# RWKV recurrence: scan states and values in two four-chunk tiles, bonus values in another pool, value stores issued by ScalarE

## The chip, the cores and the metric

The kernel runs on one core of a Trainium2 chip. The metric is device time of one launch in microseconds (us); lower is better. The core has a matrix engine (TensorE, called PE below), three engines for elementwise work (VectorE = DVE, ScalarE = ACT, GpSimd = POOL) and SyncE (SP), which here does nothing but issue DMAs. ACT can issue DMAs too. Each engine works through its own list of instructions in order and waits where a semaphore says so. A time comes with the granted TensorE clock, in parts of full speed.

## The reference

Two layers, 512 tokens, model width 1024, float32. Layer 0 has an RWKV-7 mixer, layer 1 a gated spatial unit (SGU); each is followed by a SwiGLU FFN. The change lies in the recurrence of the RWKV mixer, which runs over 16 heads of width 64:

```python
    def step(S, inp):                       # S: value x key, per head
        r_t, w_t, k_t, v_t, a_t, b_t = inp
        sa = jnp.einsum('bhij,bhj->bhi', S, a_t)
        S = (S * w_t[:, :, None, :]
             + sa[..., None] * b_t[:, :, None, :]
             + v_t[..., None] * k_t[:, :, None, :])
        y = jnp.einsum('bhij,bhj->bhi', S, r_t)
        return S, y
...
    mu = jnp.mean(y, axis=-1, keepdims=True)
    var = jnp.mean(jnp.square(y - mu), axis=-1, keepdims=True)
    y = (y - mu) * lax.rsqrt(var + GN_EPS)
    y = y * gn_w.reshape(H, N).astype(f32) + gn_b.reshape(H, N).astype(f32)
    y = y + jnp.sum(r_h * k_h * r_k.astype(f32), axis=-1, keepdims=True) * v_h
    y = y.reshape(B, T, D).astype(x.dtype)
    return (y * g) @ w_o
```

The last term before the gate, the sum over a head of r, k and r_k times the value, is called the bonus.

## The kernel before

Sixteen heads are four blocks of four heads; the 512 tokens are eight chunks of 64. For a block b the steps are: P and E (projections to r, k and the decay), F (the "front": products inside a chunk, PE lines 861 and 875, masked), B (the "back": the inverse of a 64 x 64 triangle per chunk and head; its forward substitution is a long chain of small DVE operations, lines 906 and 908, between two block transposes, LX at line 892 and Dn/Dt at lines 911 and 912), S (the scan over the eight chunks, lines 981 to 1025) and N (the "finish": group norm, bonus, output gate). V is the value projection in four column groups, lines 704 to 726. The list PLAN gives the order in which the steps are written, "P0 E0 P1 E1 P2 E2 P3 E3 X0 F0 B0 F1 V0 V1 V2 V3 B1 S0 F2 S1 F3 N0 B2 N1 B3 S2 N2 S3 N3"; a scheduler then lays the instructions of neighbouring steps into one another on every engine, by its own estimate of times and by what memory is free. So a change of a tile's place, or of the engine that issues a DMA, can move instructions that it does not name.

The value projection copies each PSUM result to a tile vev on ACT (line 724) and stores it to the array Vd in DRAM (line 725, 8 stores of 256 KB). Vd is read in two layouts. The scan reads it per chunk: a tile su holds, in its two halves of 64 partitions, the state of a head and the values of the chunk under it, so that one product applies both; its state half is written from PSUM us by DVE for one head of a pair (line 1007) and by ACT for the other (line 1010), its value half is loaded by two DMAs (line 990). The tiles su rotate through 4 buffers. The bonus reads Vd by tokens (line 1048) into a tile that shares two buffers (tag hn) with the Dn of the back and the squares of the group norm; DVE multiplies it by the bonus factor (line 1052), PE transposes it (vt, line 1055), ACT adds a bias and makes ob (line 1057). ob then takes the normalised Y (yt, line 1080) and the gate (lines 204 and 1084) and goes to DRAM as od (line 1094), from where the output projection loads it as oraw (line 1138), splits it to oT and multiplies (acc, line 204).

Weights are multiplied as a pair of roundings, whi (ACT cast, line 179) and wlo (DVE, line 180). The gate's weights g2h and g2l are made the same way from a load g (line 744); g2x (line 1069) comes from three small loads g2r (line 1066). The pool xp has four buffers of one size, given out by xslot; Y, the split input of the projections and the residual x share it. e2 gives out another pool of seven.

Of the kernel before, what the change touches and what calls it, by code (L numbers as in the profile page):

```python
# [7 lines left out]
F32 = mybir.dt.float32  # L8
# [5 lines left out]
P = 128  # L14
# [3 lines left out]
TT = T // P  # L18
H2 = 8
C = 64  # L20
# [110 lines left out]
class Trunk:  # L131
# [394 lines left out]
    def rwkv(self, x0):  # L526
        nc, i, tc = self.nc, self.i, self.tc
        v, a, g = nc.vector, nc.scalar, nc.gpsimd
        mm = nc.tensor.matmul
        with ExitStack() as ctx:  # L530
            ep = ctx.enter_context
            rp = ep(tc.tile_pool(name="rp", bufs=1))
            dp = ep(tc.tile_pool(name="dp", bufs=1, space=bass.MemoryType.DRAM))
            Vd = dp.tile([T, D], F32, name="Vd")
# [4 lines left out]
            def e(name, shape=(P, T), dt=F32):  # L539
                return rp.tile(list(shape), dt, name=name, tag="e", bufs=2)  # L540
# [4 lines left out]
            def e2(name, shape=(P, 2, T), dt=F32):  # L545
                return rp.tile(list(shape), dt, name=name, tag="e2", bufs=E2)

            def s4(name, shape, dt=F32):
                return self.slot(shape, dt, name)

            def xslot(name, shape, dt=F32):
                return self.xp.tile(shape, dt, name=name, tag="x", bufs=TT)
# [31 lines left out]
            h = [s4("h", [P, 2, 513]) for _ in range(4)]  # L584
# [3 lines left out]
            for tt in range(TT):  # L588
                hn = e2("hn", (P, D))
# [47 lines left out]
            q2 = range(2)  # L637
# [70 lines left out]
            def v_proj(xs, qts):  # L708

                for qt in qts:  # L710
                    cols = slice(qt * 256, qt * 256 + 256)
                    acc = [self.pb("v") for _ in range(2)]
                    for u in range(2):
                        hi, lo = self.weight(wrkv[2].rearrange("(u j p) n -> u p j n", p=P, j=4)[u][:, :, cols])
                        for j in range(4):
                            kt = 4 * u + j
                            for tt in range(TT):
                                tok = slice(tt * P, (tt + 1) * P)
                                self.mm3(acc[tt // 2][:, (tt % 2) * 256:(tt % 2) * 256 + 256],
                                         (xs[kt][:, 0, tok], xs[kt][:, 1, tok]), (hi[:, j, :], lo[:, j, :]),  # L720
                                         kt == 0 and tt % 2 == 0, kt == KT - 1 and tt % 2 == 1)
                    for n in range(2):
                        t = e("vev")
                        a.copy(t, acc[n])
                        nc.sync.dma_start(out=Vd.rearrange("(n j p) f -> n p j f", p=P, j=2)[n][:, :, cols],
                                          in_=t.rearrange("p (j f) -> p j f", j=2))

            fv = lambda n, p: self.vec[n][:, p:p + 1]
# [252 lines left out]
            def scan(b, o, then=None):  # L981

                MV, pc = o["MV"], o["pc"]
                Y = xslot("Y", [P, TT, 2, P])

                def new_su(c):
                    su = rp.tile([P, 2, 2, C], F32, name="su", tag="su", bufs=4)
                    vv = Vd[c * C:(c + 1) * C, 2 * b * P:2 * b * P + 2 * P].rearrange("t (q h v) -> t q h v", q=2, h=2)
                    for hd in range(2):
                        nc.sync.dma_start(out=su[64 * (1 - hd):64 * (1 - hd) + 64, :, hd, :], in_=vv[:, :, hd, :])  # L990
                        if c == 0:
                            g.memset(su[64 * hd:64 * hd + 64, :, hd, :], 0.0)
                    return su

                su = new_su(0)
                for c in range(NC):
                    hh, cc = c // 4, c % 4
                    tt, par = c // 2, c % 2
                    if c < NC - 1:
                        nsu = new_su(c + 1)  # L1000
                        us = self.bank("us", "us")
                        for q in q2:
                            for hd in range(2):
                                rows = slice(64 * hd, 64 * hd + 64)
                                mm(us[rows, q * C:(q + 1) * C], MV[hh, q][:, cc, 0, hd, :], su[:, q, hd, :], start=True, stop=True)

                        v.tensor_tensor(nsu[0:64, :, 0, :], us[0:64, 0:2 * C].rearrange("p (q v) -> p q v", q=2),
                                        pc[0:64, :, c:c + 1].broadcast_to([64, 2, C]), op=ALU.mult)
                        for q in q2:
                            a.activation(nsu[64:128, q, 1, :], us[64:128, q * C:(q + 1) * C], AF.Copy,  # L1010
                                         scale=pc[64:128, q, c:c + 1])
                    if par == 0:
                        yp = self.bank("yp", "Yp")
                    yr = slice(64 * par, 64 * par + 64)
                    for q in q2:
                        for hd in range(2):
                            yc = slice(q * P + hd * C, q * P + hd * C + C)
                            mm(yp[yr, yc], MV[hh, q][:, cc, 1, hd, :], su[:, q, hd, :], start=True, stop=True)
                    if par == 1:
                        a.copy(Y[:, tt].rearrange("p q f -> p (q f)"), yp[:, 0:2 * P])  # L1020
                    if c < NC - 1:
                        su = nsu
                    if then and c == NC // 2 - 1:
                        then(Y)
                return Y
# [18 lines left out]
            def bonus(b, o):  # L1044

                fs = slice(b * 2 * P, (b + 1) * 2 * P)
                Vn = self.sm.tile([P, TT, 2, 2, C], F32, name="hn", tag="hn", bufs=2)
                nc.sync.dma_start(out=Vn.rearrange("p t q h v -> p t (q h v)"),
                                  in_=Vd.rearrange("(t p) f -> p t f", p=P)[:, :, fs])
                obs = []  # L1050
                for q in range(2):
                    v.tensor_tensor(Vn[:, :, q], Vn[:, :, q], o["BN"][:, :, q].unsqueeze(3).broadcast_to([P, TT, 2, C]), op=ALU.mult)
                    vt = self.bank("pf", "vt")
                    for tt in range(TT):
                        nc.tensor.transpose(vt[:, tt * P:(tt + 1) * P], Vn[:, tt, q].rearrange("p h v -> p (h v)"), self.ident)
                    ob = e("ob")
                    a.activation(ob, vt, AF.Identity, bias=fv("rwkv_gn_b", 2 * b + q))
                    obs.append(ob)
                return obs
# [46 lines left out]
            for n in PLAN:  # L1106
                f, b = n[0], int(n[1])
# [181 lines left out]
```

## Time and profile before

| | us |
|---|---|
| median of 3 runs | 1358.06 (1356.09 to 1360.63) |
| the profiled execution | 1356.2 |
| its span in the trace | 1354.5 |
| PE busy, share of the span | 1285.7, 95% |
| DVE, ACT, POOL busy | 897.0, 694.1, 179.1 |
| mean granted clock | 0.979 |

The mixer takes the first 470 us or so of the span, the FFN of layer 0 the next 370, the SGU the 150 after that and the second FFN the rest. Numbers of the groups are sums over the whole span or a window; a wait is put down to what ended last. PE being busy 95% of the span does not mean that it is at full speed: the clock row says what speed was granted.

### The profile page before, as it was taken

What the parts mean: (1) busy time and instruction counts of PE and PEld (TensorE: products, weight loads), DVE (VectorE), ACT (ScalarE), POOL (GpSimd) and SP (SyncE); (2) the same over time, 40 slices, a digit from 0 to 9 for tenths busy, and PEclk for the clock granted to TensorE, in tenths of its full rate; (3) what the DMA queues carried; (4) which work ended last, traced back from release to release, by engine and by line L of the source; (5) the groups of instructions that cost most, each with busy time, mean ns of one, the idle gap of its engine ahead of it and who ended that gap; (6) DMA issues with size and microseconds to landing.
All of it is one profiled execution on the core that took longest, in us unless ns stands there. A gap on an engine that the chain in (4) does not pass through costs nothing.

```text
span 1354.5 us, 24545 instructions
## 1 busy us (share of the span) xinstructions
PE 1285.7 (95%) x9812; PEld 1116.5 (82%) x9812; DVE 897.0 (66%) x1519; ACT 694.1 (51%) x1240; POOL 179.1 (13%) x307
## 2 busy tenths in 40 slices
PE   5989999989799889999999999999989999999997
PEld 3657789887677688999998887878888999998886
DVE  7865676477847489878785225575679777785223
ACT  7975785576433375455464223643454454464221
POOL 1000175566100033000000002020002000000000
PEclk9989999999799989999999999999989999999999
DMA  5136596322214232433323332243520433323321
GB/s 158 39 85 158 135 212 176 110 74 64 85 46 136 86 102 78 125 112 107 98 78 121 93 110 80 94 148 99 157 78 16 125 109 95 109 63 124 94 93 62
DMA packets 217266, 140.10 MB, mean 103 GB/s; under 512 B 67856, under 2 KB 193344, under 8 KB 217152
## 3 DMA queue, kind: packets, MB, share of 16 engines
q1 hardware_dynamic: 215856, 133.81, 34.2%
q0 software_dynamic: 1296, 4.72, 1.0%
q8 instruction: 77, 1.26, 0.4%
q14 instruction: 37, 0.30, 0.1%
HBM read 124.35 MB, written 14.16 MB: 102 GB/s over the span
## 4 chain that ended last, share of the span: by engine, by line
PE 78%; DVE 9%; ACT 5%; DMA 4%; issue 2%; SPq 1%; POOL 0%; DVEq 0%; ACTq 0%
PE acc L204 26%; PE Q L204 10%; PE Z L204 7%; PE proj L204 6%; PE R L204 6%; PE gu L204 4%; PE u L204 3%; PE v L204 3%; PE gh L976 2%; DMA wq<-in_ffn_w_up_dram 2%; PE lm L861 2%; DVE wlo L180 2%; PE lora L649 1%; PE mp L969 1%; DVE wsum L383 1%
## 5 line engine op out<-in xcount | busy, mean ns | idle before, releaser
L180 DVE TENSOR_TENSOR wlo<-wraw,whi 128x1024 fp32r<-128x1024 f32 x109 | 133.7, 1227 | 195.4 <-ACT whi L179 191.5
L179 ACT CAST whi<-wraw 128x1024 fp32r<-128x1024 f32 x109 | 114.3, 1048 | 227.6 <-PE acc L204 142.0
L204 PE MATMUL acc<-whi,actw 128*128 128x512 f32 x704 | 220.8, 394 | 0.0
L204 PE MATMUL Q<-bc,whi 128*128 128x256 f32 x864 | 156.8, 282 | 1.7 <-ACT hn L427 1.7
L204 PEld LDWEIGHTS acc<-whi,actw 128*128 128x128 f32 x704 | 132.3, 188 | 30.6
L204 PE MATMUL acc<-wlo,actw 128*128 128x512 f32 x352 | 138.6, 394 | 0.0
L204 PEld LDWEIGHTS Q<-bc,whi 128*128 128x128 f32 x864 | 133.4, 190 | 2.5 <-ACT hn L427 2.3
L204 PE MATMUL Q<-bc,wlo 128*128 128x256 f32 x432 | 121.7, 282 | 1.1 <-DVE wlo L180 1.1
L179 ACT CAST whi<-wsum 128x1024 fp32r<-128x1024 f32 x72 | 75.2, 1051 | 84.5 <-PE Q L204 30.1
L204 PE MATMUL Z<-bc,whi 128*128 128x256 f32 x576 | 105.8, 282 | 0.7 <-ACT whi L179 0.7
L204 PE MATMUL R<-bc,whi 128*128 128x256 f32 x576 | 105.0, 281 | 0.0
L180 DVE TENSOR_TENSOR wlo<-wsum,whi 128x1024 fp32r<-128x1024 f32 x72 | 86.9, 1221 | 19.1 <-ACT whi L179 18.6
L204 PE MATMUL gu<-hT,whi 128*128 128x256 f32 (+1 forms) x384 | 92.6, 335 | 2.4 <-DVE hT L62 1.4
L204 PE MATMUL proj<-xsp,whi 128*128 128x512 f32 x256 | 85.6, 413 | 5.5 <-ACT xsp L179 3.1
L204 PEld LDWEIGHTS Z<-bc,whi 128*128 128x128 f32 x576 | 88.9, 189 | 1.1 <-ACT whi L179 0.9
L204 PEld LDWEIGHTS R<-bc,whi 128*128 128x128 f32 x576 | 88.9, 188 | 0.2
L180 DVE TENSOR_TENSOR wlo<-wq,whi 128x1024 fp32r<-128x1024 f32 x54 | 69.2, 1282 | 28.1 <-ACT whi L179 28.0
L179 ACT CAST whi<-wq 128x1024 fp32r<-128x1024 f32 x54 | 56.7, 1050 | 59.6 <-PE R L204 17.6
L204 PEld LDWEIGHTS Q<-bc,wlo 128*128 128x128 f32 x432 | 81.9, 190 | 1.5 <-DVE wlo L180 1.5
L204 PE MATMUL R<-bc,wlo 128*128 128x256 f32 x288 | 80.9, 281 | 0.0
L204 PE MATMUL Z<-bc,wlo 128*128 128x256 f32 x288 | 80.7, 281 | 0.1
L204 PEld LDWEIGHTS acc<-wlo,actw 128*128 128x128 f32 x352 | 66.1, 188 | 15.3
(346 smaller groups left out, 2858.7 us busy)
## 6 DMA issues: line engine op xcount, KB each, us to landing
wraw<-in_ffn_w_down_dram SPq DMA_DIRECT2D x44, 512.0 KB
wq<-in_ffn_w_gate_dram SPq DMA_DIRECT2D x72, 256.0 KB
wq<-in_ffn_w_up_dram SPq DMA_DIRECT2D x72, 256.0 KB
wraw<-in_rwkv_w_rkv_dram SPq DMA_DIRECT2D x24, 512.0 KB
wraw<-in_sgu_w_in_dram SPq DMA_DIRECT2D x16, 512.0 KB
x<-in_x_dram SPq DMA_DIRECT2D x8, 512.0 KB
ST<-sb SPq DMA_DIRECT2D x8, 512.0 KB
MV<-sa SPq DMA_DIRECT2D x32, 128.0 KB
```

The source lines that it names most:

```text
L179: self.nc.scalar.copy(hi, src)
L180: self.nc.vector.tensor_tensor(lo, src, hi.bitcast(F32), op=ALU.subtract)
L204: self.nc.tensor.matmul(out, l, r, start=start, stop=stop, skip_group_check=resumed)
L383: v.tensor_tensor(s, x, y, op=ALU.add)
L649: mm(acc, w1m[j][:, kt].rearrange("p j n -> p (j n)"), src(kt), start=j == 0 and kt == 0, stop=j == 1 and kt == KT - 1)
L861: mm(lm[:, cc * P:(cc + 1) * P], st[:, cc].rearrange("p n t -> p (n t)"), mv[:, cc, :, hd, :], start=True, stop=True)
L969: mm(mp[:, cc * P:(cc + 1) * P], bdT[:, q * NC + 4 * hh + cc].rearrange("p h t -> p (h t)"), mt[:, cc, :], start=True, stop=True)
L976: mm(gh[:, cc * P:(cc + 1) * P], mt[rows, cc, :], bx[rows, 0:2, cc, :], start=True, stop=True)
```

## The change

Three edits. The eight stores of the values are issued by ACT and not by SP. A scan no longer takes a tile su per chunk: it takes two tiles of four chunks each from the four xp buffers, and all value loads of a tile are issued at once, four per tile (one for each head of a pair and each of the two pairs); 64 loads of 32 KB become 32 of 64 KB. The bonus values no longer sit in the two hn buffers but in the pool that e2 gives out, with seven buffers.

```diff
@@ value projection
-                        nc.sync.dma_start(out=Vd.rearrange("(n j p) f -> n p j f", p=P, j=2)[n][:, :, cols],
+                        nc.scalar.dma_start(out=Vd.rearrange("(n j p) f -> n p j f", p=P, j=2)[n][:, :, cols],
                                           in_=t.rearrange("p (j f) -> p j f", j=2))
@@ scan
-                def new_su(c):
-                    su = rp.tile([P, 2, 2, C], F32, name="su", tag="su", bufs=4)
-                    vv = Vd[c * C:(c + 1) * C, 2 * b * P:2 * b * P + 2 * P].rearrange("t (q h v) -> t q h v", q=2, h=2)
+                sus = []
+                for c in (0, 4):
+                    t = xslot("su", [P, 4, 2, 2, C])
+                    vv = Vd[c * C:(c + 4) * C, 2 * b * P:2 * b * P + 2 * P].rearrange("(c t) (q h v) -> t c q h v", t=C, q=2, h=2)
                     for hd in range(2):
-                        nc.sync.dma_start(out=su[64 * (1 - hd):64 * (1 - hd) + 64, :, hd, :], in_=vv[:, :, hd, :])
+                        for q in q2:
+                            nc.sync.dma_start(out=t[64 * (1 - hd):64 * (1 - hd) + 64, :, q, hd, :], in_=vv[:, :, q, hd, :])
                         if c == 0:
-                            g.memset(su[64 * hd:64 * hd + 64, :, hd, :], 0.0)
-                    return su
-
+                            g.memset(t[64 * hd:64 * hd + 64, 0, :, hd, :], 0.0)
+                    sus.append(t)
+                new_su = lambda c: sus[c // 4][:, c % 4]
                 su = new_su(0)
@@ bonus
-                Vn = self.sm.tile([P, TT, 2, 2, C], F32, name="hn", tag="hn", bufs=2)
+                Vn = e2("Vn", (P, TT, 2, 2, C))
```

After the edit the lines below are numbered two higher: 990 is 992, 1007 is 1009, 1048 is 1050, 1052 is 1054, 1055 is 1057, 1069 is 1071.

The order of SP between the bonus of block 0 and the finish of block 1, before. MV are tiles of the front and back, su the scan's, hn the bonus values, od the stores of the gated output, g and g2r the gate's weights:

```order
L1048 DMA hn<-Vd 128x4x256
L845 DMA MV<-sa 64x8x64 x4
L990 DMA su<-Vd 64x2x64 x2
L845 DMA MV<-sa 64x8x64 x2
L990 DMA su<-Vd 64x2x64 x2
L1094 DMA od<-ob 128x512
L990 DMA su<-Vd 64x2x64 x2
L1094 DMA od<-ob 128x512
L990 DMA su<-Vd 64x2x64 x2
L744 DMA g_4827<-in_rwkv_g_dram 128x256
L990 DMA su<-Vd 64x2x64 x2
L1066 DMA g2r<-in_rwkv_g_dram 32x256 x3
```

The same stretch of SP with the change:

```order
L1050 DMA Vn<-Vd 128x4x256 x2
L845 DMA MV<-sa 64x8x64 x6
L1096 DMA od<-ob 128x512
L992 DMA su<-Vd 64x4x64 x8
L1096 DMA od<-ob 128x512
L744 DMA g_4785<-in_rwkv_g_dram 128x256
L1068 DMA g2r<-in_rwkv_g_dram 32x256 x3
L1050 DMA Vn<-Vd 128x4x256 x2
```

The loads for two bonuses now stand together, the second one some fifteen DMAs earlier than it did (it stood behind the oraw load and a w_o load that come after these rows), and the eight su loads of a whole scan stand in one run. The load of g stands behind the second od store in both.

The order of DVE around the end of the back of block 2, before; here g2x and g2l are the gate weights of block 1, su the state of scan 1, hn and Dt the two transposes that end the back of block 2, LX the one that begins the substitution of block 3:

```order
L1069 TENSOR_TENSOR g2x<-g2r,g2x 32x256
L908 TENSOR_TENSOR Dm<-Dm,tm 128x2x15
L1007 TENSOR_TENSOR su<-us,pc 64x2x64
L911 STREAM_TRANSPOSE hn<-Dm 128x32x32
L912 STREAM_TRANSPOSE Dt<-Dm 128x32x32
L1007 TENSOR_TENSOR su<-us,pc 64x2x64
L180 TENSOR_TENSOR g2l<-g_4827,g2h 128x256
L1007 TENSOR_TENSOR su<-us,pc 64x2x64 x2
L931 TENSOR_TENSOR Qs<-Qp,id_144 128x512
L1034 TENSOR_REDUCE mu<-Y 128x16
L892 STREAM_TRANSPOSE LX<-LA 128x1024
```

and with the change:

```order
L911 STREAM_TRANSPOSE hn<-Dm 128x32x32
L912 STREAM_TRANSPOSE Dt<-Dm 128x32x32
L1087 TENSOR_TENSOR ob<-gate,ob 128x512
L1009 TENSOR_TENSOR su<-us,pc 64x2x64
L1071 TENSOR_TENSOR g2x<-g2r,g2x 32x256
L1009 TENSOR_TENSOR su<-us,pc 64x2x64
L180 TENSOR_TENSOR g2l<-g_4785,g2h 128x256
L931 TENSOR_TENSOR Qs<-Qp,id_144 128x512
L1009 TENSOR_TENSOR su<-us,pc 64x2x64
L892 STREAM_TRANSPOSE LX<-LA 128x1024
```

g2x moves from before the two transposes to behind them, so that it stands two operations ahead of g2l; the reduction mu of the group norm moves behind LX.

The order of PE in the back of block 2, where it ends in the products T2p and mp, before (mvt and vt are transposes, Q2p a step of the inverse):

```order
L940 MATMUL Tp<-Dt,Qs 32x32 x23
L951 MATMUL Q2p<-Dn_4031,LA 32x32 x32
L919 MATMUL mvt<-ident,MV 128x128 x2
L1055 MATMUL vt<-ident,hn 128x128 x4
L919 MATMUL mvt<-ident,MV 128x128 x6
L1055 MATMUL vt<-ident,hn 128x128 x4
L960 MATMUL T2p<-bdT,Q_4071 32x32 x32
L1080 MATMUL yt<-ident,Y 128x128 x4
L969 MATMUL mp<-MVt,bdT 128x128 x4
```

and with the change:

```order
L951 MATMUL Q2p<-Dn_4003,LA 32x32 x12
L919 MATMUL mvt<-ident,MV 128x128 x4
L951 MATMUL Q2p<-Dn_4003,LA 32x32 x20
L1057 MATMUL vt<-ident,Vn 128x128 x4
L919 MATMUL mvt<-ident,MV 128x128 x16
L960 MATMUL T2p<-bdT,Q_4043 32x32 x32
L969 MATMUL mp<-MVt,bdT 128x128 x4
```

One of the two vt of block 1 now stands some twenty rows above this place, behind the last Qp of the back; the second stands right behind Q2p, no vt stands directly ahead of T2p any more, and more mvt transposes do.

## The prediction

> **What bounds the kernel now.** First the page's busy times and its chain:
>
> ```profile
> PE 1285.7 (95%) x9812; PEld 1116.5 (82%) x9812; DVE 897.0 (66%) x1519; ACT 694.1 (51%) x1240; POOL 179.1 (13%) x307
> PE 78%; DVE 9%; ACT 5%; DMA 4%; issue 2%; SPq 1%; POOL 0%; DVEq 0%; ACTq 0%
> ```
>
> The first row gives busy us and share of the span: PE sits idle for 1354.5 - 1285.7 = 69 us in the whole run. The second says who holds the chain that ended last: SP's queue 1%, transfers 4%. The change takes no work from PE, so all it can win is idle time of PE, or time at a low clock, and only between the value projection (from about 175 us) and the end of the mixer (about 475 us), where its operations stand. Next the windows of 10 us there. The columns are length, then busy time of PE, PEld, DVE, ACT, POOL, then granted clock, DMA share, GB/s:
>
> ```profile
> 180.00:190.00 10.00, 7.55 (x53) 7.38 (x52) 4.12 (x5) 9.75 (x15) 4.36 (x10) 0.83 0.94 180
> 330.00:340.00 10.00, 9.38 (x234) 7.60 (x222) 4.45 (x5) 8.35 (x23) 4.75 (x13) 1.00 0.30 79
> 340.00:350.00 10.00, 5.83 (x158) 4.60 (x155) 9.59 (x23) 5.19 (x8) 4.50 (x8) 0.83 0.51 159
> 350.00:360.00 10.00, 7.36 (x85) 6.08 (x84) 8.60 (x32) 4.15 (x6) 0.00 (x0) 0.50 0.01 2
> 360.00:370.00 10.00, 8.22 (x57) 6.90 (x55) 8.92 (x13) 1.79 (x3) 0.00 (x0) 0.84 0.25 79
> 370.00:380.00 10.00, 10.00 (x65) 8.37 (x65) 4.38 (x11) 2.58 (x5) 0.00 (x0) 0.81 0.14 42
> 440.00:450.00 10.00, 7.37 (x35) 5.85 (x36) 5.76 (x15) 3.27 (x6) 0.00 (x0) 1.00 0.52 158
> sum 330.00, PE 296.91 PEld 259.95 DVE 218.43 ACT 186.98 POOL 122.30; mean PE 9.00 PEld 7.88 DVE 6.62 ACT 5.67 POOL 3.71
> ```
>
> PE is busy 296.91 of the 330 us from 170 to 500, so at most 33 us are to be had at all. The worst stretch is 340 to 370: PE 5.83, 7.36, 8.22 while DVE is at 9.59, 8.60, 8.92, and the clock falls to 0.50. Who ended PE's idle time there and elsewhere (waits of PE, 170 to 500 us: sum, times, longest):
>
> ```profile
> PE vt L1055 <- ACT ob L1057: 3.6, 2, 2.3
> PE vt L1055 <- DVE hn L1052: 3.2, 1, 3.2
> PE lm L861 <- DMA MV<-sa: 2.4, 1, 2.4
> PE acc L204 <- ACT oT L179: 1.5, 2, 0.8
> PE yt L1080 <- ACT ob L1057: 0.8, 1, 0.8
> PE lm L861 <- DMA ST<-sb: 0.7, 1, 0.7
> ```
>
> Nobody on PE waits for a state tile's load. The transposes vt of the bonus wait most, and these the change touches.
>
> **Scan loads.** 64 issues become 32. SP spends on them (duration in ns, least, median, most):
>
> ```profile
> L990 SPq DMA_DIRECT2D su<-Vd x64: 573/599/2326, 198.3 to 424.6; - x64
> L725 SPq DMA_DIRECT2D Vd<-vev x8: 366/414/1477, 190.8 to 252.5; - x8
> SPq L990 <- PE Yp L1018: 36.3, 17, 7.7
> ```
>
> 32 x 0.599 = 19 us of SP's time go, and the waits of 36.3 us, in which SP stood still until a product had freed a tile, shrink. Both lie beside PE work, which waits for no su load; worth 0 on the path. It cannot cost there either unless a whole scan's eight loads stand before something urgent: the second tile's slot comes free when the scan before has used its last chunk, and od and g stand behind it on SP, as they stood behind single su loads. I take 0. The Trainium skill, "DMA: Bandwidth & Descriptors", section "Rules for kernel authors", tells authors to coalesce small transfers, those under 64 KB above all; 32 KB becomes just 64 KB here. By that rule alone the edit would be a gain, but the waits above show no one on PE to receive it.
>
> **Stores of the values on ACT.** Eight issues at 0.414 us are 3.3 us of ACT. On SP they no longer stand ahead of the ST loads of the second front, for which PE waited 0.7 us: at best -0.7. Against it: ACT is at 9.75 of 10 us in 180 to 190 and feeds PE with casts of the value weights and copies. Later it has room (timeline of ACT):
>
> ```profile
> 221.79 0.58 ACT L864 COPY MV<-lm 64x512 f32<-64x512 f32 x1 [3.30 <-PE lm L861]
> 235.19 1.04 ACT L179 CAST whi<-wraw 128x1024 fp32r<-128x1024 f32 x1 [3.85 <-PE v L204]
> ```
>
> It waits for PE there, 3.30 and 3.85 us at a time, so six of the eight stores should be free, and only the first two (near 191 us) meet a full ACT: 2 x 0.414 = 0.8. I take -0.7 + 0.8, near 0. Ends: -0.7, and 8 x 0.414 = +3.3 if all of it delays PE. The Trainium skill, the same page, section "Issuing engines are not separate DMA queues", says that issuing from several engines saves only the time of the issuing sequencer. This case agrees as far as it goes: it is the order on SP that is worth 0.7 us; the transfer itself would gain nothing by it.
>
> **Bonus values in their own pool.** This carries the sum. For block 1 the load waited for a free hn buffer and sat on SP behind a w_o load. How late it was (timelines of SP, DVE and PE):
>
> ```profile
> 292.75 1.35 SPq L1048 DMA_DIRECT2D hn<-Vd  x1
> 341.18 0.47 SPq L1048 DMA_DIRECT2D hn<-Vd  x1
> 346.88 0.69 DVE L1052 TENSOR_TENSOR hn<-hn,bn 128x512 f32<-128x512 f32 x1
> 347.62 1.12 PE L1055 MATMUL vt<-ident,hn 128*128 128x128 f32 x4 [3.15 <-DVE hn L1052]
> 352.31 1.11 PE L1055 MATMUL vt<-ident,hn 128*128 128x128 f32 x4 [2.29 <-ACT ob L1057]
> 353.35 1.92 PE L960 MATMUL T2p<-bdT,Q 32*32 32x32 f32 x64
> 356.67 2.08 PE L969 MATMUL mp<-MVt,bdT 128*128 128x128 f32 x8 [0.35 <-DVE bdT L964]
> ```
>
> The brackets give idle time before the row: 3.15 + 2.29 = 5.4 us. With the change this load stands right behind the first bonus load, some 48 us earlier (near the 292.75 of the first row), and the multiplications are done in the back of block 2. Both waits go. But what stands behind them on PE, mp, waits for DVE, and DVE is nearly full. So the gain is how much earlier DVE reaches the last block copy bdT (line 964), not 5.4. DVE's rows:
>
> ```profile
> 334.51 0.69 DVE L931 TENSOR_TENSOR Qs<-Qp,id 128x512 f32<-128x512 f32 x1 [0.16 <-PE Qp L928]
> 336.52 1.22 DVE L1034 TENSOR_REDUCE mu<-Y 128x16 f32<-128x1024 f32 x1 [1.32 <-ACT Y L1020]
> 337.66 1.95 DVE L892 STREAM_TRANSPOSE LX<-LA 128x1024 f32<-128x1024 f32 x1
> 345.57 1.23 DVE L180 TENSOR_TENSOR wlo<-wraw,whi 128x1024 fp32r<-128x1024 f32 x1 [0.24 <-ACT whi L179]
> 355.92 0.69 DVE L964 COPY bdT<-T2p 32x512 f32<-32x512 f32 x1 [0.74 <-ACT bdT L964]
> ```
>
> LX follows Qs (end 335.2) and one su in the new order, without mu and its wait: 335.5 where it was 337.66, that is -2.2. From LX to bdT the new order has one wlo less (-1.23), two multiplications more (2 x 0.69 = +1.4) and no wait of 0.74 for ACT: -0.6. Together -2.7. Two things in it are not seen in the trace of before. The new order also puts g2l ahead of Qs, and g2l waits for a load that SP issues only after g2x, and g2x now stands behind Dt:
>
> ```profile
> 324.68 1.90 DVE L912 STREAM_TRANSPOSE Dt<-Dm 128x1024 f32<-128x1024 f32 x1
> 323.84 0.54 SPq L744 DMA_DIRECT2D g<-in_rwkv_g_dram  x1
> 327.65 0.42 DVE L180 TENSOR_TENSOR g2l<-g,g2h 128x256 fp32r<-128x256 f32 x1 [0.95 <-ACT g2h L179]
> ```
>
> From issue to g2l took 3.8 us. Dt ended at 326.6; with ob and su g2x would start near 327.6 and end at 328.0, and g2l comes at 331.9 to 333, still ahead of Qs, which waits for PE's Qp until 334.5. So this wait is covered, by 1.5 us or more. And two bonus blocks' multiplications and a pair of ob move into the back of block 2, which pushes its Dt back by up to 2 us. I keep -2.7; the ends are 0 (Dt late, LX where it was) and, with both waits gone and nothing in their place, -5.4.
>
> Whether the clock recovers is a term of its own. By the windows PE ran at half clock for all of 350 to 360, and, read from 0.84 and 0.81, for 3.2 us of the next window and 3.8 us of the one after. Up to mp at 356.7 the slow PE hides behind DVE; after it (3.3 + 3.2 + 3.8) / 2 = 5.2 us are lost. In the new order the work that PE has between Q2p and mp is still the two groups vt and mvt, T2p and yt, 5 us or so at full clock in a stretch of 10, so PE stays half idle, and I count 0, with an end of -5.2.
>
> **The tail.** The bonus of block 3 had its transposes behind the last scan, where ACT was busy with casts (timeline of PE):
>
> ```profile
> 441.09 0.66 PE L1055 MATMUL vt<-ident,hn 128*128 128x128 f32 x4 [1.29 <-ACT ob L1057]
> 442.53 0.44 PE L1080 MATMUL yt<-ident,Y 128*128 128x128 f32 x2 [0.78 <-ACT ob L1057]
> 443.73 0.50 PE L204 MATMUL acc<-whi,oT 128*128 128x512 f32 x1 [0.76 <-ACT oT L179]
> ```
>
> In the new order these vt stand inside the scan, and the od of block 2 that oT waits for is written before the scan's last steps. 1.29 + 0.78 + 0.76 = 2.8 us; I take -2.3, since part of such a gap has moved elsewhere each time above. Ends 0 and -2.8.
>
> Sum: 0 + 0.1 - 2.7 - 2.3 = -4.9 us against the profiled execution, 1356.2, which lies 1.9 under the median. Against the median of 1358.06: **1353**. A difference of 0.3%, 4.1 us, is what a measurement of this kernel can tell from no change.
>
> **The rivals.**
>
> *The stall only changes its place* (0.26). DVE holds the back of block 3, 9.59 and 8.60 of 10 us, and if the work moved into the back of block 2 delays Dt by the 2 us above, LX is where it was; then the tail's 2.3 alone are left, or less: 1356. For it speaks that DVE, not the transfer, is full there; against it that mu and its wait of 1.32 leave the path.
>
> *Idle and clock both go* (0.18). If PE's idle time between 344 and 357 falls apart into short pieces, the clock stays up: -5.4 - 5.2 - 2.8 + 0.1 = -13.3, so 1345. For it: the clock fell just at the 3.15 and 2.29 us gaps, and the scan's tiles are loaded long before use. Against it: DVE's share. The Trainium skill, "TensorE: Matmul & The Clock Gate", section "HAM oscillation — how this bites in real kernels", warns of idle gaps over about 3.4 us; here 0.50 began with gaps of 3.15 and 2.29, so the trace is a little stricter, and by that rule pieces under that length would give this case.
>
> *ACT's queue is held* (0.13), the slower side. One mechanism: in the program each DMA waits for an earlier one on its semaphore, and the eight stores then take not 0.414 but the 1.477 us of the slowest row or more, in a stage whose DMA share is 0.94 (180 to 190); behind them on ACT stand the casts whi and the copies MV, LA, BX for which PE's v, lm and bkt wait. 8 x 1.477 = 11.8 us, less the cover that ACT's idle gives for half of them: +6 to +9 there, and with the gains halved 1358 + 7 - 2 = 1363. It decides once ACT loses more than the 3.3 us it has to wait for PE. Against it: on SP six of the eight took near the median.
>
> *The scan's steps stand too close* (0.07), slower as well. In the new order some steps of scan 2 (us, Yp, us) have nothing between them, so that PE would wait for the state from DVE and ACT at each. One such exchange at 0.5 us, for six to eight chunks, is +3 to +4 beside the gains: 1357 to 1362. Before, fronts and output products lay between most of them.
>
> **How the numbers follow.** Forecast 1353 with 0.36, no change 0.26, the large gain 0.18, ACT held 0.13, close steps 0.07. The forecast's own band is 1350 to 1356. The 8-in-10 range reaches from 1344 (the large gain) to 1363 (ACT held). Faster than 1354.0: four fifths of the forecast's share (0.29), the large gain (0.18) and a little of the no-change case (0.03): 0.50. Slower than 1362.1: ACT held (0.13), half of the close steps and a little of the others: 0.21. The rest, 0.29, lies within 0.3%.
>
> **What would show it.** Right: no PE vt row with an idle time over 1 us; both Vn issued near 293; LX of block 3 before 337; mp of the back of block 2 at 353 to 355; no gap ahead of acc near 440. Wrong: PE idle at T2p or mp as long as it was at vt (the second case); the clock at 1.00 through 340 to 375 (the third); ACT rows at line 725 over a microsecond, or v, lm and bkt waiting for ACT between 185 and 255 (the fourth); a wait of DVE at g2l that ends after Qp.

## The result, and the profile after

| | before | after |
|---|---|---|
| median of 5 runs each, us | 1358.06 (1355.38 to 1360.63) | 1370.69 (1369.30 to 1375.96) |
| ratio, 95% interval | | 1.0106 (1.0078 to 1.0133) |
| the profiled execution, its span | 1356.2, 1354.5 | 1369.3, 1367.6 |
| mean granted clock of the profiled execution | 0.979 | 0.971 |

The change makes the kernel slower by 1.1%. The forecast was 1353, and the range ended at 1363. The busy times and the chain of the changed kernel's page:

```profile
span 1367.6 us, 24430 instructions
PE 1297.8 (95%) x9812; PEld 1127.5 (82%) x9812; DVE 900.8 (66%) x1519; ACT 694.8 (51%) x1240; POOL 174.2 (13%) x307
PE 82%; DVE 10%; ACT 3%; DMA 2%; issue 2%; SPq 1%; DVEq 0%; ACTq 0%
```

PE does the same 9812 products as before, but is busy 1297.8 us where it was 1285.7: 12.1 more. Its idle time is 1367.6 - 1297.8 = 69.8 us and was 68.8. So PE does not wait longer; the same products take longer. That points at the granted clock: (1 - 0.971) x 1367.6 = 39.7 us of the span are lost to it, against (1 - 0.979) x 1354.5 = 28.4 before, a difference of 11.3 out of 13.1.

Where the clock is lost is seen in the windows of 10 us that the prediction read before (length, busy time of PE, PEld, DVE, ACT, POOL, granted clock, DMA share, GB/s), here of the changed kernel:

```profile
340.00:350.00 10.00, 5.49 (x114) 4.63 (x115) 9.84 (x21) 7.50 (x11) 1.80 (x5) 0.87 0.20 66
350.00:360.00 10.00, 7.30 (x57) 6.64 (x54) 9.73 (x34) 1.16 (x2) 0.00 (x0) 0.50 0.06 13
360.00:370.00 10.00, 8.83 (x41) 7.13 (x40) 6.00 (x12) 3.35 (x6) 0.00 (x0) 0.67 0.11 41
370.00:380.00 10.00, 10.00 (x45) 8.60 (x46) 3.55 (x7) 0.62 (x2) 0.41 (x2) 0.50 0.09 30
380.00:390.00 10.00, 10.00 (x189) 8.59 (x190) 4.06 (x10) 3.28 (x9) 0.00 (x0) 0.59 0.18 54
```

Up to 360 the rows look as before. From 370 to 390 PE is busy all the time, 10.00 of 10 us, at a clock of 0.50 and 0.59, where before it had 0.81 in 370 to 380. A busy time of 10.00 reads like an engine at its best; the clock beside it says that half of it is lost. Cut at the moments at which the clock changes (the last row of each ends at 398.50 in both), the same stretch reads so, first before, then after:

```profile
346.60:360.20 13.60, 9.94 (x94) 8.08 (x94) 11.97 (x42) 4.75 (x8) 0.00 (x0) 0.50 0.13 40
360.20:367.10 6.90, 5.12 (x41) 4.34 (x41) 6.65 (x9) 1.17 (x2) 0.00 (x0) 0.99 0.36 114
367.10:373.90 6.80, 6.80 (x32) 6.02 (x31) 3.75 (x8) 2.60 (x5) 0.00 (x0) 0.50 0.00 0
373.90:398.50 24.60, 22.23 (x587) 18.45 (x586) 9.94 (x22) 9.26 (x23) 0.18 (x1) 1.00 0.18 55
```

```profile
347.30:361.00 13.70, 9.53 (x100) 8.88 (x100) 13.37 (x41) 3.94 (x6) 0.00 (x0) 0.50 0.14 49
361.00:364.40 3.40, 2.23 (x16) 1.66 (x16) 3.37 (x7) 0.86 (x2) 0.00 (x0) 1.00 0.02 8
364.40:388.30 23.90, 23.90 (x219) 20.07 (x221) 8.37 (x20) 5.64 (x13) 0.41 (x2) 0.50 0.08 26
388.30:398.50 10.20, 8.06 (x328) 6.90 (x319) 3.22 (x6) 4.55 (x10) 0.00 (x0) 1.00 0.35 98
```

The first loss, 13.6 and 13.7 us, is in both, and there PE waits for DVE anyway. After a short return to 1.00 the clock falls again in both: before for 6.8 us, after for 23.9, in which PE never stands still. Each of these stretches at 0.50 is a multiple of 3.4 us within the reading (2, 4 and 7 times). PE's timeline of the changed kernel over this stretch (brackets: idle time ahead of the row, and what ended it):

```profile
348.77 1.92 PE L960 MATMUL T2p<-bdT,Q 32*32 32x32 f32 x64 [2.84 <-ACT bdT L945]
352.65 2.08 PE L969 MATMUL mp<-MVt,bdT 128*128 128x128 f32 x8 [1.97 <-DVE bdT L964]
...
362.42 0.33 PE L1007 MATMUL us<-su,MV 128*64 128x64 f32 x2 [1.16 <-DVE MV L978]
...
363.01 1.16 PE L976 MATMUL gh<-BX,MVt 64*128 64x128 f32 x8
...
375.12 2.07 PE L976 MATMUL gh<-BX,MVt 64*128 64x128 f32 x8
...
386.79 1.80 PE L928 MATMUL Qp<-hn,LA 32*32 32x32 f32 x128
```

Eight products gh take 1.16 us at 363.01 and 2.07 at 375.12. mp begins at 352.65, where before it began at 356.67: the part that the change aimed at came 4.0 us early. Qp of block 3, at 381.81 before, begins at 386.79, 5.0 late. So 9.0 us are lost between the two. The clock accounts for it: from mp to Qp PE ran at 0.50 for 3.5 + 6.8 = 10.3 us before and for 8.3 + 22.4 = 30.7 after; half of the difference is 10.2. The whole stretch from mp to Qp, first before, then after, says the same:

```profile
356.67:381.81 25.14, 23.02 (x148) 19.24 (x149) 17.34 (x37) 6.58 (x14) 0.00 (x0) 0.79 0.18 55
```

```profile
352.65:386.79 34.14, 32.24 (x153) 27.32 (x153) 19.29 (x45) 6.55 (x13) 0.41 (x2) 0.55 0.08 26
```

PE's idle time in it is 2.1 us before and 1.9 after; all of the 9.0 us is busy time, at a clock of 0.55 where it was 0.79.

The product us at 362.42 stands in the 3.4 us ahead of the long stretch at 0.50, behind 1.16 us of waiting for MV. DVE's timeline of the changed kernel says why MV came late:

```profile
334.99 1.92 DVE L892 STREAM_TRANSPOSE LX<-LA 128x1024 f32<-128x1024 f32 x1 [0.32 <-POOL LA L829]
...
358.08 2.03 DVE L911 STREAM_TRANSPOSE hn<-Dm 128x1024 f32<-128x1024 f32 x1
359.99 1.92 DVE L912 STREAM_TRANSPOSE Dt<-Dm 128x1024 f32<-128x1024 f32 x1
361.94 0.42 DVE L978 TENSOR_TENSOR MV<-gh,BX 128x256 f32<-128x256 f32 x1
```

The two block transposes of block 3 (hn is here the name of Dn's buffer), 4 us of DVE, are ahead of the small addition for which the scan waits. They were ahead of it before too (DVE, then PE, of the kernel before):

```profile
362.29 2.07 DVE L911 STREAM_TRANSPOSE hn<-Dm 128x1024 f32<-128x1024 f32 x1
364.27 1.89 DVE L912 STREAM_TRANSPOSE Dt<-Dm 128x1024 f32<-128x1024 f32 x1
366.03 0.38 DVE L978 TENSOR_TENSOR MV<-gh,BX 128x256 f32<-128x256 f32 x1
```

```profile
366.51 0.30 PE L1005 MATMUL us<-su,MV 128*64 128x64 f32 x2 [1.48 <-issue]
```

The view names no releaser for these 1.48 us ("issue"), but they end 0.1 us behind the end of MV at 366.41. So the wait alone does not explain the longer loss; the experiments below take it up.

After the mixer the kernel is 7.3 us behind (first FFN product, gu, at 486.5 where it was at 479.2), 10.7 at the first SGU product (wst, 849.46 and 838.75), and 13.1 at the end.

### The profile page after: what moved, and what is told of

Read it like the earlier page. It is cut to its first block, busy times and chain, and to the rows that moved or that the text cites. A ratio compares the mean times of both kernels' runs of the same rounds, so it can differ in the third digit from the quotient of the medians.

```text
span 1367.6 us, 24430 instructions
## 1 busy us (share of the span) xinstructions
PE 1297.8 (95%) x9812; PEld 1127.5 (82%) x9812; DVE 900.8 (66%) x1519; ACT 694.8 (51%) x1240; POOL 174.2 (13%) x307
## 4 chain that ended last, share of the span: by engine, by line
PE 82%; DVE 10%; ACT 3%; DMA 2%; issue 2%; SPq 1%; DVEq 0%; ACTq 0%
PE acc L204 27%; PE Q L204 10%; PE Z L204 7%; PE R L204 6%; PE proj L204 6%; PE gu L204 4%; PE u L204 3%; PE v L204 3%; PE gh L976 2%; PE lm L861 2%; DVE wlo L180 2%; PE lora L649 1%; DVE wsum L383 1%; PE mp L969 1%; PE Yp L1020 1%
## 5 line engine op out<-in xcount | busy, mean ns | idle before, releaser
L204 PEld LDWEIGHTS acc<-whi,actw 128*128 128x128 f32 x704 | 132.2, 188 | 30.7
```

Of the source, the lines that this page charges most:

```text
L204: self.nc.tensor.matmul(out, l, r, start=start, stop=stop, skip_group_check=resumed)
```

## The experiments

Two theories were put against each other first. The clock: the new order leaves PE idle in small pieces among narrow products, and the clock is lost for longer. The edits: one of the three costs something itself (stores that hold ACT, loads that come in a block, multiplications on a full DVE). To weigh them, "lost to the clock" below is (1 - granted clock) x span, averaged over all executions of a kernel, and "rest" is the mean time without it; this counts a slow clock in full even where PE would have waited, so it is a book-keeping and no time on the path. Each group of experiments ran beside the kernel before, whose median was 1356.9 to 1358.5.

### Each edit alone

Of the kernel before, one edit each. The diffs are the three hunks of the change: the line 725 alone; the tiles su alone; the tile Vn alone.

> Only the stores of the values move to ScalarE; scan tiles and bonus values stay as before. Theory A (the loss is PE time at half clock between 346 and 388 us, brought by the new order of the back of block 2 and scan 2): this edit alone gives none of it, 1355 to 1360, mean granted clock 0.977 or more. Theory B (the stores hold ScalarE's queue in the value projection): 1364 to 1370, with the loss between 185 and 255 us. B is already weak, since in the changed kernel the value projection ends at 250.7 us as before.

> Only the scan's states and values go to two four-chunk tiles in the xp buffers. Theory A: if the half clock comes with the packed order of scan 2, which these tiles allow, this edit carries most of the loss: 1364 to 1372 at a clock of 0.970 to 0.973. Rival A2 (the half clock comes from the bonus values' own pool, which moves the vt transposes): 1356 to 1361 at 0.977 or more.

> Only the bonus values move to the pool of seven. By the rival A2: 1364 to 1372 at a clock of 0.970 to 0.973. If the half clock belongs to the scan's tiles: 1352 to 1359, the idle time of 5.4 us ahead of vt gone and most of it back at T2p and mp.

Measured, against 1358.45 for the kernel before: stores on ACT 1358.14, ratio 0.999 (0.997 to 1.0009); scan tiles 1358.25, 0.9988 (0.9969 to 1.0008); bonus pool 1356.17, 0.9981 (0.9959 to 1.0004). None of the three costs anything alone, and their ratios multiply to 0.996, not to 1.011. The loss is in the combination. Theory B is out, and so is the guess that the scan tiles (1364 to 1372) or the bonus pool alone would carry it.

### Two edits at a time

```diff
 # e5_no_act: the change without its first edit
-                        nc.scalar.dma_start(out=Vd.rearrange(...)
+                        nc.sync.dma_start(out=Vd.rearrange(...)
 # e6_no_su: the change with the scan tiles of before (new_su, 4 buffers)
-                    t = xslot("su", [P, 4, 2, 2, C])
+                    su = rp.tile([P, 2, 2, C], F32, name="su", tag="su", bufs=4)
 # e7_no_vn: the change with the bonus values in the buffers hn
-                Vn = e2("Vn", (P, TT, 2, 2, C))
+                Vn = self.sm.tile([P, TT, 2, 2, C], F32, name="hn", tag="hn", bufs=2)
```

> The changed kernel with the stores of the values back on SP: scan tiles and bonus pool together. Each edit alone gave 1356 to 1358, so the loss needs a pair. Theory A (the scan tiles and the bonus pool together make the order in which PE waits once in the back of block 2 and then runs narrow products at half clock up to 388 us): 1366 to 1372, clock 0.969 to 0.972. Rival (the stores on ScalarE are needed for it): 1354 to 1359, clock 0.977 or more.

> Stores on ScalarE and bonus pool, scan tiles as before. Theory A: the scan tiles are missing, so 1354 to 1359. Rival: 1366 to 1372.

> Stores on ScalarE and scan tiles, bonus values in the two old buffers. Theory A: the bonus pool is missing, so 1355 to 1360. Rival: 1366 to 1372.

Against 1356.94 before: without the ACT stores **1354.68, ratio 0.9968 (0.9945 to 0.9991)**; without the scan tiles 1362.64, 1.0035 (1.0005 to 1.0066); without the bonus pool 1359.83, 1.0019 (1.0000 to 1.0037). So taking the stores off ACT repairs all of it, though the stores alone cost nothing, and though nothing around them is slower in the changed kernel: the last value product stands at 250.7 there and at 250.8 before. The pair that was expected to carry the loss, scan tiles with bonus pool, is the one without it: this kernel is faster than the change and, by 0.3%, than the kernel before. Its windows, cut at its clock's changes:

```profile
343.70:357.30 13.60, 10.18 (x146) 8.92 (x146) 13.23 (x42) 4.53 (x7) 1.69 (x4) 0.50 0.14 41
357.30:384.60 27.30, 24.78 (x531) 21.08 (x532) 18.82 (x44) 12.95 (x28) 0.41 (x2) 1.00 0.30 87
```

The first loss is the same 13.6 us; the second is not there. (A loss of 6.8 us begins at 384.6, among Tp and Q2p; the change has one of 3.4 us at the same work, at 398.5.) And its DVE and PE (timelines):

```profile
358.03 0.42 DVE L978 TENSOR_TENSOR MV<-gh,BX 128x256 f32<-128x256 f32 x1 [0.27 <-PE gh L976]
364.85 2.08 DVE L911 STREAM_TRANSPOSE hn<-Dm 128x1024 f32<-128x1024 f32 x1
```

```profile
359.39 0.70 PE L204 MATMUL gate<-sg,g2h 128*128 128x512 f32 x2
360.50 0.34 PE L1007 MATMUL us<-su,MV 128*64 128x64 f32 x4
```

Here MV is done ahead of the transposes, us does not wait, and the wide products of the gate stand ahead of it; in the changed kernel gate came at 368.28, when the clock was already down. Two things could be the cause, then: the order MV / transposes, or the place of the wide products.

In the kernel without the scan tiles the clock stood at 0.50 for 34.2 us without a break, while PE was idle for 3.8 of them:

```profile
349.20:383.40 34.20, 30.42 (x185) 25.92 (x184) 23.64 (x60) 6.75 (x11) 0.00 (x0) 0.50 0.12 40
```

That is one execution, of 1372.43 us; the executions of this kernel spread from 1357.91 to that, and their granted clocks from 0.981 to 0.967. An order does not fix the clock alone.

### More work for PE

Two kernels fill PE with dummy products whose results are overwritten. One puts 10 products of 128x512 ahead of T2p and 8 ahead of the first mp of block 2, where PE waits; the other puts 2 ahead of each group gh of block 2, so that narrow products have wide ones among them.

```diff
+def fill(mm, sg, t, n):
+    for _ in range(n):
+        mm(t, sg[:, 0, 0:P], sg[:, 0, :], start=True, stop=True)
 # e4_filled
+                T2p = self.bank("pt", "T2p"); fill(mm, sg, T2p, 10 if b == 2 else 0)
+                    ... fill(mm, sg, mp, 8 if (b == 2) and (hh, q) == (0, 0) else 0)
 # e8_wide_gh
+                        gh = self.bank("pt", "gh"); fill(mm, sg, gh, 2 if b == 2 else 0)
```

> The changed kernel, with dummy products of 128x512 in the back of block 2: ten into the bank of T2p before its own products and eight into the bank of mp, which they leave overwritten, so that PE stays busy in the idle 2.84 and 1.97 us there. They are PE work of 18 x 0.24 = 4.3 us. Theory A, if the idle time sets off the low clock: the clock stays at 1.00 through 347 to 388, up to 11 us come back, 1358 to 1364. If the low clock is not set off by this idle time, or the loss is not the clock's at all: 1371 to 1375.

> The changed kernel with two dummy products of 128x512 ahead of each of the eight gh of the back of block 2, into the same bank, overwritten after: 16 x 0.24 = 3.8 us more PE work at full clock, spread over the stretch of narrow products from 354 to 387 us. Theory A in its sharper form (once down, the clock stays down as long as the windows of 3.4 us hold only narrow products such as gh, us, Yp and mvt, and comes back with wide ones): the long stretch at 0.50 shrinks from 23.9 us to 7 or less, 8 us or more come back against 3.8 us of work, 1361 to 1368. If the low clock has nothing to do with the kind of products: 1373 to 1380.

Filled waits: 1362.96, ratio 1.0033 (1.0005 to 1.0061), so with some 4 us of work added the kernel is 7.7 us faster than the change; in mean, the loss to the clock falls from 43.0 to 32.9 us and the rest rises from 1329.2 to 1332.0. But its profiled execution, of 1372.49 us, does not show what was expected of the clock: the first loss is down to 3.4 us, and a second of 20.5 us follows, with PE busy throughout:

```profile
372.90:393.40 20.50, 20.50 (x224) 17.43 (x223) 7.78 (x19) 8.08 (x18) 0.00 (x0) 0.50 0.21 54
```

Wide products among gh: 1372.5, 1.011 (1.0066 to 1.0154): the loss to the clock falls too, to 34.6, but the rest rises by 9.0, and nothing is won. Its profile also shows why it is no clean experiment: us waited there for MV not 1.16 but 3.38 us, and 0.50 followed for 20.5 us. In those 20.5 us wide products stood among the narrow ones, in nearly every 3.4 us some, and the clock stayed where it was; so some wide products among narrow ones do not bring it back. Both kernels have another order than the change on all engines, and neither says which wait it is.

### The order alone

These kernels add no work and take none away. A constraint makes one DVE instruction stand behind another on the same engine, with no semaphore. The first is the change with both transposes of block 3 forced behind the first four MV additions of block 2's back, as the kernel without ACT stores has them by itself.

```diff
 # e9_mv_first; last holds (block, addition), behind(x, [y]) puts x after y on its engine
-                v.transpose(Dn..., full(Dm)...)
-                v.transpose(Dt..., full(Dm))
+                behind(tc, v.transpose(Dn..., full(Dm)...), [x for y, x in last if b == 3 and y == 2][1:2])
+                behind(tc, v.transpose(Dt..., full(Dm)), [x for y, x in last if b == 3 and y == 2][1:2])
```

> The changed kernel with one constraint of order on VectorE: the four additions MV of the first unit of the back of block 2 stand ahead of the two transposes Dn and Dt of block 3, not behind them. No work and no wait is added; the rest of the order stays nearly as it was. In the changed kernel PE's first us of scan 2 waited 1.16 us for these MV at 361.3, the clock fell to 0.50 at 364.4 and stayed there for 23.9 us. Theory C (this wait sets off the long stretch at half clock): the wait is gone, the stretch at 0.50 after 361 goes or shrinks to 7 us, 1357 to 1363, clock 0.975 or more. Rival (the stretch comes from the kind and order of PE's products alone, whatever sets it off): 1368 to 1374, clock 0.969 to 0.972.

1360.11, ratio 1.0017 (0.9996 to 1.0039), 10.6 us less than the change and no longer told from the kernel before. Its executions (1354.99 to 1364.45) lie all below those of the change (from 1369.30). The loss to the clock falls from 43.0 to 31.2 us in mean, the rest stays (1328.5 and 1329.2). In its trace (PE, then the windows at the clock's changes):

```profile
362.28 0.97 PE L1082 MATMUL yt<-ident,Y 128*128 128x128 f32 x4
363.18 0.34 PE L1007 MATMUL us<-su,MV 128*64 128x64 f32 x4
```

```profile
352.80:363.00 10.20, 7.69 (x36) 7.11 (x36) 9.90 (x32) 1.62 (x3) 0.00 (x0) 0.50 0.14 49
363.00:386.90 23.90, 21.73 (x476) 18.19 (x478) 14.09 (x29) 10.43 (x25) 0.41 (x2) 1.00 0.28 78
```

us has no bracket: the wait is gone, and the clock stays up for the 23.9 us for which it was down in the change. The gates still come behind the product us here (366.57), so their place does not explain it. The rest of the trace is not all better: ahead of this product 17.0 us run at 0.50 (6.8 from 342.6 and the 10.2 shown), and another 6.8 begin at 386.9.

The counter-test takes the good kernel, without ACT stores, and forces its first MV behind the transpose Dt.

```diff
 # e10_mv_late, on e5_no_act
-                v.transpose(Dt..., full(Dm))
+                ahead(tc, v.transpose(Dt..., full(Dm)), [x for y, x in last if b == 3 and y == 2][0:1])
```

> The opposite, in the kernel with scan tiles and bonus pool but stores on SP, 1354.7: the first MV of the back of block 2 is forced behind the transpose Dt of block 3 on VectorE, so that the first us of scan 2 must wait as it does in the changed kernel. Theory C: an idle time of 1 us or more ahead of us, the clock at 0.50 for 7 to 24 us behind it, 1359 to 1368. Rival (this wait does not matter): 1353 to 1357.

1368.76, ratio 1.0089 (1.0060 to 1.0119), 14.1 us more than the kernel that it was made from. The loss to the clock goes from 26.5 to 42.7 us, the rest from 1328.0 to 1326.1. PE and the windows:

```profile
367.28 1.16 PE L976 MATMUL gh<-BX,MVt 64*128 64x128 f32 x8 [0.60 <-DVE MV L979]
369.38 0.34 PE L1007 MATMUL us<-su,MV 128*64 128x64 f32 x4 [0.95 <-DVE MV L978]
378.51 1.56 PE L976 MATMUL gh<-BX,MVt 64*128 64x128 f32 x8 [1.72 <-DVE MV L979]
```

```profile
379.00:385.90 6.90, 6.25 (x32) 4.92 (x31) 2.33 (x5) 5.72 (x12) 0.00 (x0) 0.51 0.22 54
396.10:409.80 13.70, 12.73 (x227) 11.62 (x227) 5.02 (x9) 5.68 (x15) 0.00 (x0) 0.50 0.20 60
```

The waits for MV are back, but they do not act as expected. No fall follows the 0.95 us ahead of the product us, nor the 0.60 ahead of gh; one follows the 1.72 us, and the MV awaited there stands behind another operation than the transposes (DVE):

```profile
377.27 0.42 DVE L180 TENSOR_TENSOR g2l<-g,g2h 128x256 fp32r<-128x256 f32 x1 [2.15 <-ACT g2h L179]
377.95 0.41 DVE L979 TENSOR_TENSOR MV<-gh,MV 128x256 f32<-128x256 f32 x1
```

The 13.7 us begin in a gap of 1.86 us ahead of Tp, and the first loss is 17.1 us (from 344.9) where the good kernel has 13.6. So the counter-test shows that order alone, with no work added, costs 14.1 us, and that all of it is clock; it does not show that the wait ahead of the product us is what costs it.

### The bonus multiplications held back

One more on the good kernel: the multiplications Vn of blocks 2 and 3 stay behind the last bdT copy of block 2's back, to see what a DVE with less to do ahead of mp is worth.

```diff
 # e11_vn_late, on e5_no_act
-                    v.tensor_tensor(Vn[:, :, q], Vn[:, :, q], o["BN"]..., op=ALU.mult)
+                    behind(tc, v.tensor_tensor(Vn[:, :, q], Vn[:, :, q], o["BN"]..., op=ALU.mult), [x for y, h, x in last if b >= 2 and y == 2 and h == 1])
```

> The kernel with scan tiles and bonus pool and the stores on SP (1354.7), with the four multiplications of the bonus values of blocks 2 and 3 (2.9 us of VectorE) held behind the last bdT copy of the back of block 2 on VectorE. They stood between LX of block 3 and the bdT copies for which PE's T2p and mp wait (idle 1.16 and 2.26 us there). If that chain is what PE waits for: mp 2 to 3 us earlier, 1351 to 1354. If the additions MV are pushed late by it, as in the changed kernel: the clock falls again behind us, 1356 to 1366.

1365.62, ratio 1.0058 (1.0033 to 1.0083): worse by 10.9 us than the kernel it was made from. mp began at 354.15, where the good kernel has it at 353.55, so the held work did not free the path; instead yt waited 1.95 us for DVE, and the loss to the clock rose from 26.5 to 34.8 us, the rest from 1328.0 to 1331.6. The time lies just in the range of the second case, but not by its mechanism: the product us, at 363.69, does not wait, and 20.5 us at 0.50 run from 344.0. As a way to a faster kernel it is a miss.

### All of them together

The medians of the first two rows are those of the result; the means of the kernel before are over the 31 executions beside the single edits.

| kernel | median, us | mean, us | lost to the clock | rest |
|---|---|---|---|---|
| before | 1358.06 | 1358.0 | 31.6 | 1326.4 |
| after | 1370.69 | 1372.2 | 43.0 | 1329.2 |
| stores on ACT alone | 1358.14 | 1358.1 | 32.8 | 1325.3 |
| scan tiles alone | 1358.25 | 1357.4 | 29.6 | 1327.8 |
| bonus pool alone | 1356.17 | 1356.2 | 28.6 | 1327.6 |
| without ACT stores | 1354.68 | 1354.6 | 26.5 | 1328.0 |
| without scan tiles | 1362.64 | 1364.4 | 34.2 | 1330.2 |
| without bonus pool | 1359.83 | 1359.9 | 34.8 | 1325.1 |
| waits filled | 1362.96 | 1364.8 | 32.9 | 1332.0 |
| wide products among gh | 1372.50 | 1372.9 | 34.6 | 1338.2 |
| MV ahead of the transposes | 1360.11 | 1359.8 | 31.2 | 1328.5 |
| good kernel, MV behind | 1368.76 | 1368.8 | 42.7 | 1326.1 |
| good kernel, Vn held | 1365.62 | 1366.4 | 34.8 | 1331.6 |

Of the 14.2 us between the means of before and after, 11.4 are the clock and 2.8 the rest. Where no dummy work is added, the rest stays between 1325.1 and 1331.6 and the clock's part between 26.5 and 43.0.

## Why the prediction was wrong, step by step

**The scan's loads, 0: nothing against it.** No wait of PE for su's loads appears, and the edit alone gives 0.9988.

**The stores on ACT, near 0: right in what it priced, wrong as a whole.** The eight issues on ACT took 0.37 to 0.41 us, last v ended where it did, and the edit alone gives 0.999. Nothing of "ACT's queue is held" happened, whose 1363 also lay under the result. What the step left out is that the edit shifts a schedule: beside the other two edits it is the difference between 1354.68 and 1370.69. The text in front of the prediction says that a tile's place or an issuing engine can move instructions that an edit doesn't name; the sum gave that no term.

**The bonus pool, -2.7: right, a little small.** Both Vn loads were issued at 288 to 298, as predicted. LX was predicted at 335.5 and came at 334.99; mp was predicted at 353 to 355 and came at 352.65, 4.0 earlier than before. The waits of PE at vt are gone, and in their place PE waits at T2p and mp, as five rows of the waits from 170 to 510 us show (sum, times, longest):

```profile
PE mp L969 <- DVE bdT L964: 3.9, 2, 2.0
PE T2p L960 <- ACT bdT L945: 2.8, 1, 2.8
PE us L1007 <- DVE MV L978: 1.5, 2, 1.2
PE acc L204 <- ACT oT L179: 2.1, 1, 2.1
PE vt L1057 <- ACT ob L1059: 0.3, 1, 0.3
```

This is the sign that was named for "the stall only changes its place", and it misled: 2.84 + 1.97 us of idle time stand there for 5.44 at vt, and yet mp came 4.0 earlier. The argument that the gain is how much earlier DVE gets to bdT held; the sign did not tell it apart from the rival. The g2l wait was covered, as worked out: it ended at 332.26, Qs came at 333.09.

**The clock after mp, "I count 0, with an end of -5.2": the step that failed.** It asked only whether the lost 5.2 us would come back. The other side, that the same kind of loss could grow, had no term, no rival and no end in the range. (The bound of "at most 33 us" has the same gap: it counts idle time alone, while PE at 0.50 counts as busy.) The premise that PE stays half idle up to mp was right (5.49 and 7.30 of 10), and up to there the loss stayed as it was. What failed is the part behind it: from mp to Qp the half clock went from 10.3 to 30.7 us, 10.2 us of time, where 0 was put. The order experiments show the cause in part: with the same work, MV ahead of the transposes takes away the wait ahead of the product us, the fall behind it and 10.6 us, and another order on DVE puts 14.1 us of clock on the good kernel, but by other waits. They do not show why the fall behind the product us cost two slots of 3.4 us before and seven after. The place of the wide products alone does not answer it: before, the clock came back behind a slot that held eight mp and two gate products, but in the change four gate products stood in the second of the seven and again in the sixth, and it stayed down. What the traces say of such slots, counted over all kernels, stands at the end.

**The tail, -2.3: right where it looked, and given back behind it.** Ahead of the vt and acc at 440 to 444 only 0.22 to 0.30 us of idle time are left, where there were 2.8 us. But further on, at 470.36, acc now waits 2.12 us for oT (before, two gaps of 0.73 and 1.15 stood near there), and a half clock of 3.4 us begins at 470.2.

**The sum.** -4.9 was predicted, +13.1 came, 18.0 apart. In order of time: up to mp it went 1.3 us better than predicted; from mp to Qp 9.0 were lost where 0 was put, which the clock accounts for; from Qp to first gu 2.3 were lost where -2.3 was put, so 4.6; from there to the end 5.8 where nothing was put. Of these last, the idle times of PE over 0.25 us make up 3.7 (15.5 in sum after gu, 11.8 before; the largest new ones are 1.98 us ahead of ptr at 497.36 and 2.88 ahead of Q at 1068.77), while the half clocks in that stretch are about as long as before. No experiment took this part apart; it stays open.

**The rivals.** The steps of the scan that stand too close were nearest in place: the loss begins within 3.4 us of the product us. But it was priced as an exchange of state with DVE and ACT, 0.5 us each, and those waits are small (Yp waits 0.7 us at most). The wait that counts in the change is for MV, behind two transposes, and its price is not the wait but the clock behind it.

The Trainium skill, "TensorE: Matmul & The Clock Gate", section "HAM oscillation — how this bites in real kernels", was read in the prediction as a length of gap to stay under, about 3.4 us. The runs differ: 0.50 followed gaps of 1.16 (here) and 1.72 us (the counter-test), while 0.60 and 0.95 did nothing there; the counts at the end go by PE's busy time in a slot of 3.4 us and not by the length of one gap. The section "What's actually happening" of "Part 1: The HAM clock gate" of the same page has the full clock back after one busy window of about 3.4 us; here PE was busy for 23.90 of 23.90 us at 0.50. It also says that the windows run freely and don't start with the kernel. The traces agree: the clock changes on a grid of 3.413 us, whose first edge lies 0.2 to 3.1 us behind the start of the span. That could make executions of one order differ, as those of the kernel without scan tiles do, but each kernel has one trace, so no run here shows it.

## What to carry to other kernels

Read the granted clock beside the busy time, and where it is already lost in a stretch, give the loss a term with both signs: 20 us at half clock cost 10 us, more than any wait that this change touched. In a scheduled program the smallest edit is also a new order; compare what the order does at the narrow places (here, which small operation stands behind a 2 us transpose on an engine that PE waits for), and try the edits in all their combinations before keeping or dropping them: the two that are good together were hidden by a third that is free alone. An order constraint without a wait is a cheap experiment. It can be a repair (10.6 us here), but it is a new order too, and two of the three tried here made their kernel slower, one of them meant as a gain.

## What the runs showed of the hardware

A PE that is busy without a gap does not by that get its clock back: 23.9 us at 0.50 in the change, 20.5 with filled waits, and nearly as long in the kernel with wide products among gh (its windows):

```profile
366.90:387.30 20.40, 20.40 (x78) 16.38 (x77) 5.94 (x13) 2.76 (x5) 0.41 (x2) 0.50 0.04 14
```

In each of the thirteen traces the clock changes only on a grid of 3.413 us, to within 2 ns; the time from one edge of the grid to the next is called a slot here. So one fall costs at least half a slot, 1.7 us, where PE is the bound, and seven times as much where it stays down as in the change.

The falls go by PE's busy time in a slot, so by its idle time summed, not by the length of one gap. Counted over all thirteen traces, each of the 142 falls came behind a slot in which PE was busy for 2.50 us or less. All 96 slots at full clock with less than 1.55 us had a fall behind them; of the 154 between, 46 had. In the change, the slot with the wait ahead of the product us (361.0 to 364.4) had 2.25 us and a fall; in the counter-test, 365.4 to 368.8 had 2.31 and none.

The returns go with the size of the products. In 159 slots at half clock PE was busy for 3.35 us or more. Behind 43 of them the clock stayed down, and in none of these was a product of the full 128*128 under way for more than 2.37 us; behind 116 it returned, and 104 of these had more than 2.4. The products gh are 64*128, us and Yp 128*64. The first six of the seven slots in the change had 1.5 to 1.9 us of full products; before, the slot of the return (370.5 to 373.9) had 2.5. The seventh in the change had 0.1 us of them, most of the rest being us, Yp and the 32*32 products Qp, and the clock returned, so this is not the whole rule. These are counts over traces and no experiment: no kernel here changes the size of the products alone.
